# Two superblocks of 2 x 2 quadrants for o and pg over all tokens, with W_o's and W_pg's quadrant sums kept split in DRAM

## The chip, the cores and the metric

The kernel runs on 1 core of one Trainium2 chip. The metric is device time in microseconds (us), measured over the whole execution. Five engines take part: TensorE (PE) for matrix products, with its own sequence of weight loads (PEld); VectorE (DVE), ScalarE (ACT) and GpSimd (POOL) for elementwise work; SyncE (SP), which here only issues DMAs. POOL's queue also issues DMAs, among them those that add into their target (accumulate). The clock that is granted to PE is shown by the profile as a share of full speed (PEclk).

## What is computed

One layer over 2048 prompt tokens and 32 sample tokens with 1024 features, in float32:

```python
z = rmsnorm(x) @ W_in          # q | k | v | gate A | B | C | conv in | conv gate | merge A | merge B
q, k = rope(rmsnorm(q)), rope(rmsnorm(k))        # 8 query heads, 2 key heads of 64
attn = softmax with a sink per head, each chunk of 64 tokens sees itself and 2 chunks before it
yA = (attn * silu(gate_A)) @ W_A                 # 512 -> 1024
yB = (B * conv3(C * u) * silu(gate_C)) @ W_B     # 512 -> 1024
r = x + (sigmoid(mA) * yA + sigmoid(mB) * yB) @ W_o
out = r + sigmoid(r @ W_pg) * (p @ W_pp)         # p has 256 features
```

Besides out, the last rows of k, v and of the conv input are returned.

## The kernel before

Features lie on the 128 partitions and tokens along the free axis. Each float32 operand is split into a high part `hi`, rounded to the matmul format (fp32r), and the rest `lo`; a product is three matmuls, hi·hi, hi·lo and lo·hi, summed in PSUM. The split of a weight piece (128 x 512, 256 KB) is a CAST on ACT and a subtraction on DVE, and the result takes one of `WB` = 5 buffers `w` (hi and lo side by side, 512 KB). Raw pieces come through 8 buffers `wr`.

The program has three phases. Phases 1 and 2 (about 30 to 440 and 440 to 860 us of the span) make `x @ W_in` in two halves of the tokens by Strassen's scheme as Winograd arranges it: 7 products of quadrants in place of 8, for 21 groups of output features. During phase 1, `quad_sums` (L355) loads the four quadrants of W_o and W_pg for each of 4 output rows, makes the 4 sums of quadrants that the scheme needs (products 7, 5, 6 and 3), and stores these 32 sums to DRAM as `qs`, unsplit, for use in phase 3.

Phase 3 (`run_units`, L2247, from about 862 us) works through a list of units written as `plan` (L273 to L287): `yB` and `yA` (products with W_B and W_A, by block of tokens and output row n), `pp` (p @ W_pp for blocks 2 and 3; the others are made earlier), and the two big products `o` (with W_o, key `UO` = 50 in names) and `pg` (with W_pg, `UPG` = 58). Tokens are in four blocks (`BLOCKS`, L23): 512, 512, 512 and 512 + 32, the sample tile being part of the last. o and pg are made in three ways:

- block 0: plainly, 8 x 8 pieces, units `o` and `pg` (`done_o`, `done_pg`);
- blocks 1 and 2: as one superblock (`BIG`, units of kind "B") by the scheme of 7 products, each quadrant 512 features by the 512 tokens of one block; `big_x` makes the 7 combinations of rows, `run_big` the products, `big_done` combines the results and `big_end` finishes a row (for o: add xT by an accumulating DMA and store to `z_r`, the result staying in SBUF as pg's operand; for pg: tanh, times pp, add z_r by an accumulating DMA, store to the output);
- block 3: the same scheme within the block, quadrants of 272 tokens (units of kind "S": `row_quads`, `run_quads`, `quad_done`, `o_quad`, `pg_quad`; tiles `rq`, `s50`, `s58`), in an order of products written out by hand in `last_parts` and `last_pg`.

Attention runs beside the units: 17 tiles of 128 tokens (`attention`, L1330), of two chunks each. A chunk goes through S (scores), E (exp), P (normalised), PT (transposes), O (output); at most two P are live. When the last tile of a block is stored to `z_at`, rows are loaded back (`acf`), split into `ac` and used by yA of that block. The times at which tiles begin are set in a list `begin` (L2300 to L2317), by units of planned PE work.

The order of all this is decided when the program is built: each operation goes through a helper (`call`, L121) that adds its estimated cost (`cost`, L100) to a clock of its engine, `go` starts a generator whose steps become due at such times, and between two matmuls `due` (L172) starts whatever is due and fits in the free buffers (`limit`, L90). PE's own sequence is therefore: units in the order of `plan`, with attention's matmuls put in where they fall due. `next_loads` (L2203) issues weight loads up to 11 pieces ahead (`LOOK`), in the order `worder`, and `split_w` splits them. All operations recorded by the helper have one line in the profile: L135 before, L136 in the changed kernel.

## Time and profile before

| | |
|---|---|
| time, median of 3 runs | 1522.86 us (1521.79 to 1523.18) |
| time of the profiled execution | 1523.18 us |
| its span | 1521.4 us |
| PE, PEld busy | 99%, 88% of the span |
| DVE, ACT, POOL busy | 79%, 55%, 24% |
| DMA from SP's queue | 251.84 MB |
| DMA from POOL's queue | 85.99 MB |
| granted PE clock, mean | 0.993 |

The page lists busy times by engine, the span in slices, the DMA queues, the chain of work that ended last and the costliest groups. Matmuls are pipelined, so a busy share of 99% doesn't say that PE is at its peak: the pitch of instructions in a window in which PE never pauses tells what one costs. A row such as `wr<-qs SPq DMA_DIRECT2D x64, 256.0 KB, 4.8` gives the number of issues, the size of each and the median time from issue to landing. In the view of waits a row names the waiting operation and the engine and tile that it waited for, then the total, the number of times and the longest, in us.

### The profile page before, as it was taken

How to read it: one execution, taken by the hardware profiler on the slowest of the kernel's cores; microseconds unless marked ns; L12 is line 12 of the kernel's file. 1: busy time of each engine (PE TensorE's matmuls, PEld its weight loads, DVE VectorE, ACT ScalarE, POOL GpSimd, SP SyncE). 2: the span in 40 equal slices, each digit the busy share in tenths (PEclk: the TensorE clock that was granted, in tenths of full speed). 3: DMA queues.
4: the chain of work that ended last, by engine and by line, in shares of the span. 5: the costliest groups of instructions: out<-in, count | busy, mean ns of one | idle time of the engine just before them, and what ended most of it. 6: DMA issues, size and time to landing. Idle time of an engine off the chain costs nothing. (4 is left out here: it accounts for less than half of the span.)

```text
span 1521.4 us, 27059 instructions
## 1 busy us (share of the span) xinstructions
PE 1501.7 (99%) x9025; PEld 1334.0 (88%) x9025; DVE 1205.0 (79%) x2291; ACT 835.1 (55%) x1964; POOL 370.3 (24%) x533
## 2 busy tenths in 40 slices
PE   9999999999999999999999999999999999999898
PEld 7878888888889999999999989978888888889898
DVE  7897887875579776898965788789887699786786
...
GB/s 343 152 273 342 310 300 221 286 337 273 245 278 260 322 153 197 110 129 123 153 193 188 254 328 221 221 214 229 193 205 213 240 131 175 275 171 298 272 309 258
DMA packets 207004, 357.39 MB, mean 235 GB/s; under 512 B 24592, under 2 KB 61520, under 8 KB 206864
## 3 DMA queue, kind: packets, MB, share of 16 engines
q1 hardware_dynamic: 164928, 251.84, 51.0%
q0 software_dynamic: 32288, 85.99, 19.6%
...
HBM read 238.21 MB, written 117.46 MB: 234 GB/s over the span
## 5 line engine op out<-in xcount | busy, mean ns | idle before, releaser
L599 PE MATMUL a<-x_l,w 128*128 128x264 f32 (+1 forms) x744 | 228.2, 319 | 0.0
L597 PE MATMUL a<-x_h,w 128*128 128x264 f32 (+1 forms) x744 | 227.2, 320 | 0.0
L602 PE MATMUL a<-x_h,w 128*128 128x264 f32 (+1 forms) x744 | 201.4, 320 | 0.4 <-DVE w L207 0.4
L206 ACT CAST w<-wr 128x512 fp32r<-128x512 f32 (+1 forms) x180 | 110.1, 619 | 104.7 <-PE c L602 28.8
L135 ACT CAST w<-wr 128x512 fp32r<-128x512 f32 x204 | 124.6, 620 | 75.5 <-PE yA L135 17.7
L207 DVE TENSOR_TENSOR w<-wr,w 128x512 fp32r<-128x512 f32 (+1 forms) x180 | 133.8, 753 | 35.2 <-ACT w L206 33.3
L135 DVE TENSOR_TENSOR w<-wr,w 128x512 fp32r<-128x512 f32 x204 | 139.7, 693 | 21.4 <-ACT w L135 18.5
L599 PEld LDWEIGHTS a<-x_l,w 128*128 128x128 f32 x744 | 140.0, 188 | 10.3
L597 PEld LDWEIGHTS a<-x_h,w 128*128 128x128 f32 x744 | 139.7, 188 | 10.4
L135 PE MATMUL b<-xb_h,w 128*128 128x512 f32 x448 | 142.0, 394 | 0.0
L602 PEld LDWEIGHTS a<-x_h,w 128*128 128x128 f32 x744 | 125.2, 188 | 11.2 <-DVE w L207 0.6
L735 PE MATMUL la<-x_h,w 128*128 128x264 f32 x516 | 111.8, 285 | 1.6 <-ACT w L206 1.0
L597 PE MATMUL c<-x_h,w 128*128 128x512 f32 (+1 forms) x336 | 110.5, 339 | 0.1
L599 PE MATMUL c<-x_l,w 128*128 128x512 f32 (+1 forms) x336 | 110.4, 338 | 0.0
L206 ACT CAST w<-a 128x512 fp32r<-128x512 f32 x82 | 49.7, 620 | 95.5 <-DVE a L346 33.2
L602 PE MATMUL c<-x_h,w 128*128 128x512 f32 (+1 forms) x336 | 99.9, 338 | 0.0
L135 PEld LDWEIGHTS b<-xb_h,w 128*128 128x128 f32 x448 | 83.6, 188 | 17.9
L796 DVE SCALAR_TENSOR_TENSOR u<-u,c 128x264 f32<-128x264 f32 (+1 forms) x125 | 59.4, 506 | 43.8 <-ACT u L791 27.3
L135 PE MATMUL yA<-ac_h,w 128*128 128x512 f32 (+1 forms) x320 | 90.4, 360 | 2.3 <-ACT ac_h L135 1.8
L791 ACT COPY u<-a 128x264 f32<-128x264 f32 (+1 forms) x114 | 47.4, 437 | 80.8 <-PE a L602 72.5
L735 PEld LDWEIGHTS la<-x_h,w 128*128 128x128 f32 x516 | 87.0, 189 | 2.2 <-ACT w L206 1.2
L135 PE MATMUL b<-xb_l,w 128*128 128x512 f32 x224 | 88.5, 395 | 0.0
...
## 6 DMA issues: line engine op xcount, KB each, us to landing
wr<-in_wu SPq DMA_DIRECT2D x213, 256.0 KB, 4.1
a<-in_wu SPq DMA_DIRECT2D x116, 256.0 KB, 5.1
wr<-ws SPq DMA_DIRECT2D x74, 256.0 KB, 3.4
wr<-qs SPq DMA_DIRECT2D x64, 256.0 KB, 4.8
ws<-a POOLq DMA_DIRECT2D x63, 256.0 KB, 4.0
qs<-a POOLq DMA_DIRECT2D x24, 256.0 KB, 5.8
tb<-z_t SPq DMA_DIRECT2D x24, 256.0 KB, 4.4
z_t<-tb SPq DMA_DIRECT2D x24, 256.0 KB, 4.0
```

The source lines that it names most:

```text
L135: return f(**kw)
L206: nc.scalar.copy(out=hi, in_=src)
L207: nc.vector.tensor_tensor(out=lo, in0=src, in1=hi.bitcast(F32), op=sub)
L597: nc.tensor.matmul(out=ps[:, :cn], lhsT=w[:, 0, k], rhs=x[0][:, c0:c0 + cn], start=first and k == 0, stop=False, skip_group_check=True)
L599: nc.tensor.matmul(out=ps[:, :cn], lhsT=w[:, 0, k], rhs=x[1][:, c0:c0 + cn], start=False, stop=False, skip_group_check=True)
L602: nc.tensor.matmul(out=ps[:, :cn], lhsT=w[:, 1, k], rhs=x[0][:, c0:c0 + cn], start=False, stop=k == 3, skip_group_check=True)
L735: nc.tensor.matmul(out=ps[:, :m], lhsT=w[:, a, k], rhs=r[:, cols], start=q in "ABG" and j == 0 and e == 0, stop=j == 1 and e == 2, skip_gr ...
L791: nc.scalar.copy(out=t[:, c0:c0 + cn], in_=ps[:, :cn])
L796: nc.vector.scalar_tensor_tensor(out=t[:, c0:c0 + cn], in0=t[:, c0:c0 + cn], scalar=-1.0, in1=ps[:, :cn], op0=mul, op1=sub)
```

## The change

All tokens now go through superblocks: blocks of 512, 512, 528 and 528 tokens (the sample tile stands between prompt tiles 11 and 12, at the border of the two last blocks, and belongs to both), and two superblocks s = 0 (blocks 0 and 1, 512 wide) and s = 1 (blocks 2 and 3, 528 wide, each product in two parts of 264). The plain units `o`, `pg` and the quadrants within block 3 are removed. yB comes for all four blocks first (each W_B piece once), then pp for blocks 2 and 3, then yA, o and pg of superblock 0, then those of superblock 1. Pieces of W_A and W_pp are loaded raw and split for each block that uses them. The order of products is changed so that the results chain differently: product 6 gives c12, product 7 takes it from there to c21, and so on (`BO`, `BIG_AFTER`). In s = 1 the last rows of pg add r from SBUF ("rs") on DVE in place of an accumulating DMA.

`quad_sums` splits each of its 32 sums (a CAST on ACT into a tile of the new tag "kh", a subtraction on DVE in place) and stores both parts, 64 stores; it runs at the steps of groups 3, 5, ..., 17 in place of 1 to 8. At use, `next_loads` loads a sum's two parts with one DMA of 512 KB straight into a buffer `w`, with no split. There are 64 such loads, as many as there were raw loads of sums.

```diff
-BLOCKS = [(0, 512, 0), (512, 512, 0), (1024, 512, 0), (1536, 512, TS)]
+BLOCKS = [(0, 512), (512, 512), (1024, 528), (1552, 528)]
+TILES = [(P * i, P) for i in range(12)] + [(T3, TS)] + [(T3 + TS + P * i, P) for i in range(4)]
-W = 512 + TS
+W = 532
...
-    BIG = (1, 2)
-    BO = {UO: (2, 7, 1, 6, 5, 3, 4), UPG: (1, 7, 6, 5, 3, 2, 4)}
...
+    BO = {UO: (2, 1, 6, 7, 5, 3, 4), UPG: (1, 6, 7, 5, 3, 2, 4)}
+    NA = [((4, 5, 6, 7, 0, 1, 2, 3), (0, 4, 1, 5, 2, 6, 3, 7))[b % 2] for b in range(NB)]
+
+    def products_of(s_, x):
+        def pairs_of(p, r):
+            return [("B", s_, x, n, v) for e in (0, 2) for v in (p, r) for n in (e, e + 1)]
+        out = {p: [("B", s_, x, n, p) for n in range(4)] for p in (2, 7, 4)}
+        out[5] = pairs_of(5, 3)
+        if x == UPG:
+            out[1] = pairs_of(1, 6)
+        else:
+            out.update({p: [("B", s_, x, n, p) for n in range(4)] for p in (1, 6)})
+        return [v for p in BO[x] if p in out for v in out[p]]
+
+    plan = [("yB", b, n) for n in range(2) for b in range(3)] + [("yB", 3, n) for n in range(2)]
+    plan += [("yB", b, n) for n in range(2, 8) for b in range(4)]
+    first, second = products_of(0, UO), products_of(1, UO)
+
+    def mixed(b, parts):
+        ys = [("yA", b, n) for n in NA[b]]
+        return ys[:6] + [parts[0], ys[6], parts[1], ys[7]] + parts[2:]
+
+    pps = [("pp", 3, n) for n in range(8)]
+    plan += [("pp", 2, n) for n in range(8)] + pps[:4] + [("yA", 0, n) for n in NA[0]]
+    plan += first[:4] + pps[4:] + mixed(1, first[4:8]) + first[8:] + products_of(0, UPG)
+    plan += [("yA", 2, n) for n in NA[2]] + second[:4] + mixed(3, second[4:8]) + second[8:] + products_of(1, UPG)
...
-    quad_sum = {(x, n): dram.tile([P, 4, 4, P], F32, tag=f"qs{x}_{n}", name=f"qs{x}_{n}") for x in (UO, UPG) for n in range(4)}
+    quad_sum = {(x, n): dram.tile([P, 4, 2, 4 * P], F32, tag=f"qs{x}_{n}", name=f"qs{x}_{n}") for x in (UO, UPG) for n in range(4)}
...
         for p, o in ((7, "sc"), (5, "a21"), (6, "a11"), (3, "a12")):
-            nc.gpsimd.dma_start(out=quad_sum[x, n][:, WS[p]], in_=t[o])
+            h, lo = high(f"qh{p}_{x}_{n}"), t[o].bitcast(F32R)
+            split(h, lo, t[o])
+            nc.gpsimd.dma_start(out=quad_sum[x, n][:, WS[p], 0], in_=h.bitcast(F32))
+            nc.gpsimd.dma_start(out=quad_sum[x, n][:, WS[p], 1], in_=t[o])
...
-    sums_at = {(0, 1 + 2 * n + e, 6): (x, n) for n in range(4) for e, x in enumerate((UO, UPG))}
+    sums_at = {(0, 3 + 2 * (n + 4 * e), 6): (x, n) for n in range(4) for e, x in enumerate((UO, UPG))}
...
+    def ac_rows(b, j):
+        while b not in ac_open:
+            yield {}
+        yield {"tmp": 1}
+        yield from split_rows(0.5, lambda: ac_pair(b, j), z_at[:, j], ("ac", b, j), b)
...
+        if "rs" in u:
+            eV.tensor_tensor(out=t, in0=t, in1=u["rs"][:, :m], op=add)
...
+        subs = blk(2 * s)[2]
+        floor[0] = 3 * len(subs)
+        fresh = p != 3 and (p != 6 or x == UO)
...
+        for y, (ps, c0, cn) in enumerate(pss):
+            for k in range(4):
+                while ("XB", s, x, p, k) not in have or w_ready.get(wi, 1e9) > now[0]:
                     idle()
...
+                w = wp.tile([P, 2, 4, P], F32R, tag="w", name=f"w{i}")
+                W2[i] = w[:, 0], w[:, 1]
+                fin[0] = 0.0
+                eY.dma_start(out=w.bitcast(F32).rearrange("p a b c -> p a (b c)"), in_=quad_sum[key[2:4]][:, WS[key[4]]])
+                w_ready[i] = fin[0] + 0.5
...
-    e1, e2 = T[f"yA1_{NA[1][0]}"], T["yA3_0"]
+    e1, e2 = T[f"yA1_{NA[1][0]}"], T[f"yA2_{NA[2][0]}"]
+    left.update({0: 4, 1: 4, 2: 5, 3: 5})
+    for e in range(len(TILES)):
+        t = 11 * e if e < 8 else e1 - 30 + (e2 - e1) * (e - 8) / 9
+        begin.append((t, lambda e=e: go(attention(e), None, {"z": 1, "tmp": 2})))
```

In PE's sequence, at the end of the attention of block 1 (chunks 14 and 15 are its last; names are tile, chunk and a running number), these rows stood before, block 0's plain `o0` among them:

```order
L135 MATMUL O_15_13021<-ptl_15_2_12916,VH_10072 128x256
L135 MATMUL o0_3_0_12962<-m0_7_h_12698,w395_12841 128x512
L135 MATMUL pq2_2_13037<-cst_69,zq2_2_12828 128x128 x4
L135 MATMUL pkv2_2_13042<-cst_69,zkv2_2_12830 128x128 x2
L135 MATMUL o0_4_0_13049<-m0_0_h_12298,w396_12868 128x512
L135 MATMUL PT_16_0_13062<-cst_69,P16_12804 128x128 x4
L135 MATMUL PT_16_2_13069<-cst_69,P16_12804 128x128 x2
L135 MATMUL o0_4_0_13049<-m0_0_l_12299,w396_12868 128x512
L135 MATMUL S_18_0_13083<-KH_10068,qs2_1_12983 128x192
```

At the same place in the changed kernel, PE has the next three chunks without other work between them, and then yA of block 1:

```order
L136 MATMUL O_15_13235<-ptl_15_2_13186,VH_10224 128x256
L136 MATMUL PT_16_0_13249<-cst_69,P16_13080 128x128 x4
...
L136 MATMUL S_18_0_13271<-KH_10220,qs2_1_13221 128x192
...
L136 MATMUL O_16_13291<-pth_16_0_13254,VH_10224 128x256
...
L136 MATMUL PT_17_0_13304<-cst_69,P17_13193 128x128 x4
...
L136 MATMUL O_17_13347<-pth_17_0_13309,VH_10224 128x256
...
L136 MATMUL PT_18_0_13361<-cst_69,P18_13270 128x128 x4
...
L136 MATMUL O_18_13389<-ptl_18_2_13372,VH_10224 128x256
L136 MATMUL yA1_0_0_13144<-ac1_0_h_13379,w385_12870 128x512
```

The 512-wide matmuls of o that stood between the chunks are gone from here, and yA1, which stood behind all of block 0's o and pg, follows directly.

On DVE, the last rows of the program (the last combinations of pg's products with pp and with r) were these:

```order
L135 TENSOR_TENSOR e33_3_18105<-e33_3_18105,s58d_3_18302 128x272
L135 SCALAR_TENSOR_TENSOR tg133_3_18235<-tg133_3_18235,pp133_3_18233 128x272
L135 TENSOR_TENSOR tg133_3_18235<-tg133_3_18235,rs133_3_18237 128x272
...
L135 SCALAR_TENSOR_TENSOR tg033_3_18165<-tg033_3_18165,pp033_3_18163 128x272
L135 TENSOR_TENSOR tg033_3_18165<-tg033_3_18165,rs033_3_18166 128x272
```

In the changed kernel they are:

```order
L136 TENSOR_TENSOR c21_158_2_7_18101<-c21_158_2_7_18101,rs2_2_18621 128x528
L136 TENSOR_TENSOR c21_158_3_7_18146<-c21_158_3_7_18146,b158_3_4_0_18724 128x264
L136 TENSOR_TENSOR c21_158_3_7_18146<-c21_158_3_7_18146,b158_3_4_1_18725 128x264
L136 SCALAR_TENSOR_TENSOR c21_158_3_7_18146<-c21_158_3_7_18146,pp2_3_18656 128x528
L136 TENSOR_TENSOR c21_158_3_7_18146<-c21_158_3_7_18146,rs2_3_18658 128x528
```

The last product is combined in two parts of 264, and the steps behind it take a whole row of 528 columns where they took 272.

More of the change, by code (lines that the diff above doesn't have):

```diff
@@ L1382, in attention @@
             eS.copy(out=h, in_=src)
-        if last and i >= 3:
+        if out:
             vo = tmp(f"vo{i}", cols=P)
@@ L1412, in attention @@
         yield {"ps": 2, "qs": 1}
-        if last and i >= 3:
+        if out:
             ko = kso[P - TS:P] if sample else kpo
@@ new lines, in big_unit @@
+            if s and (n == 3 and p in (2, 4) or p == 4):
+                loads.append(("rs", z_r[n + 4 * i]))
+        units.append(dict(b=2 * s + j, n=n, p=p, x=x, s=s, kind="B", name=f"b{s}{x}_{n}_{p}", w=[("B", s, x, n, p)],
+                          act=[()] * 4, loads=loads, got=0))
+    def run_big(u):
+        s, x, n, p = u["s"], u["x"], u["n"], u["p"]
+        g = big[s, x, n]
+        subs = blk(2 * s)[2]
+        floor[0] = 3 * len(subs)
+        fresh = p != 3 and (p != 6 or x == UO)
+        if not fresh:
+            while ("e", s, x, n, {6: 1, 3: 5}[p]) not in have:
+                idle()
+        if fresh:
+            pss = []
+            for e, (c0, cn) in enumerate(subs):
@@ L2079, in run_quads @@
                 banks[0] += 1
-                g[new] = bank(f"s{x}{new}_{n}")
-        for k in range(4):
-            for (n, p), wk in zip(u["parts"], u["w"]):
-                wi = w_of(wk, u)
-                i, half = XP[p]
-                while ("X", x, i, k) not in have or w_ready.get(wi, 1e9) > now[0]:
+                pss.append((bank(f"b{s}{x}_{n}_{p}_{e}"), c0, cn))
+            if p in (1, 5):
+                g["a"] = pss
+        else:
+            pss = g["a"]
+        wk, = u["w"]
@@ L2091, in run_quads @@
-                if k == 3 and p in (1, 5, 6):
-                    hold[0] = now[0] + 0.2 + SEM + 3 * (0.00044 * m + 0.0064)
-                for e, (w, r) in enumerate(((hi, xs[0]), (hi, xs[1]), (lo, xs[0]))):
-                    eT.matmul(out=ps[:, :m], lhsT=w, rhs=r, start=fresh and k == 0 and e == 0, stop=k == 3 and e == 2,
-                              skip_group_check=True)
-                    due()
-                if k == 3:
-                    w_over(wk)
-        for n, p in u["parts"]:
-            go(quad_done(x, n, p), now[0] + SEM, None, -1)
+                xh, xl = XB[s, x, p, k]
@@ new lines, in run_big @@
+                for e, (w, r) in enumerate(((hi, xh), (hi, xl), (lo, xh))):
+                    while begin and begin[0][0] <= work[0]:
+                        begin.pop(0)[1]()
+                    eT.matmul(out=ps[:, :cn], lhsT=w, rhs=r[:, c0:c0 + cn], start=fresh and k == 0 and e == 0,
+                              stop=k == 3 and e == 2, skip_group_check=True)
+                    work[0] += 0.00044 * cn + 0.0064
+                    due()
+                if n == 3 and y == len(pss) - 1:
+                    free("k", 2)
+                    free("kx", 2)
@@ L2169, in tile_hybrid_stream_step @@
     room = {"w": WB - len(W2), "wf": 8}
-    n_load, to_split, landed = [raws[0]], list(range(len(made), raws[0])), {i: 3.0 for i in range(raws[0])}
-    room["wf"] -= len(to_split)
+    n_load, n_split, landed = [raws[0]], [len(made)], {i: 3.0 for i in range(raws[0])}
+    room["wf"] -= raws[0] - len(made)
     def w_of(key, u):
```

681 lines of the change are left out of this document (176 added, 505 removed).

## The prediction

> **What bounds the kernel now.** I read the busy shares first, then TensorE's (PE's) list of waits, then windows.
>
> ```profile
> span 1521.4 us, 27059 instructions
> PE 1501.7 (99%) x9025; PEld 1334.0 (88%) x9025; DVE 1205.0 (79%) x2291; ACT 835.1 (55%) x1964; POOL 370.3 (24%) x533
> ```
>
> PE is busy for all but 20 us, so the time is the sum of its instructions, plus the few places where it stops. The execution took 1523.18 us, 1.8 more than its span; the median of the runs is 0.3 below it. What an instruction costs is its pitch, read where PE never pauses. The next rows hold start and end, then busy time with instruction counts for PE, its weight loads (PEld), DVE, ACT and POOL, then the granted clock, the DMA share and GB/s.
>
> ```profile
> 160.00:200.00 40.00, 40.00 (x175) 32.43 (x174) 32.30 (x53) 15.92 (x35) 11.85 (x24) 1.00 0.90 311
> 600.00:640.00 40.00, 40.00 (x331) 40.00 (x330) 29.42 (x57) 16.11 (x36) 11.09 (x16) 1.00 0.34 106
> 1441.00:1470.00 29.00, 29.00 (x234) 29.00 (x233) 23.13 (x46) 19.87 (x41) 5.21 (x6) 1.00 1.02 302
> ```
>
> The first holds 512-wide matmuls, 40.00/175 = 228.6 ns each; the second 264-wide ones, 120.8 ns; the third 272-wide ones, 123.9 ns. Two halves of 264 cost 241.6 ns, so half a superblock of 528 columns costs 13 ns more than one of 512. Where PE stops is in the next two views: waits (total, times, longest), and windows at the attention output of block 0 and at the start of the quadrants of block 3.
>
> ```profile
> PE s50a L135 <- DVE w L135: 2.5, 1, 2.5
> PE yA L135 <- ACT ac_h L135: 1.8, 2, 1.3
> PE s50b L135 <- DVE w L135: 1.4, 1, 1.4
> ...
> 995.00:1010.00 15.00, 11.91 (x48) 8.15 (x46) 9.56 (x23) 10.52 (x31) 0.00 (x0) 0.66 0.50 163
> 999.40:1009.70 10.30, 9.19 (x26) 6.02 (x27) 5.14 (x11) 5.88 (x17) 0.00 (x0) 0.50 0.30 115
> 1420.00:1440.00 20.00, 15.38 (x99) 14.40 (x98) 17.62 (x34) 10.87 (x22) 2.62 (x3) 0.83 0.80 228
> 1440.00:1500.00 60.00, 59.33 (x468) 58.54 (x467) 51.54 (x102) 41.09 (x87) 12.07 (x14) 1.00 0.99 305
> ```
>
> The list shows single waits of 1 to 2.5 us; the windows show what they cost with the clock that falls behind them. At 995 to 1010, PE is idle for 15.00 - 11.91 = 3.1 us, and of the 9.19 busy us at clock 0.50 half, 4.6, is lost: **7.7 us**. At 1420 to 1440, 99 matmuls at 123.9 ns are 12.3 us: **7.7 us** lost; in the 60 us after it 468 are 58.0: **2.0 us**.
>
> **The matmuls.** Counted in the order of both kernels, 624 of 512 columns and 1152 of 272 go, 2304 of 264 come: block 0's plain o and pg (384 of 512) fall under the scheme, while blocks 2 and 3 turn 528 wide. At the pitches: -142.6 - 142.7 + 278.3 = **-7.0 us**. The arithmetic saved for block 0 is nearly all spent on the 264-wide halves. Here the Trainium skill speaks: "TensorE: Matmul & The Clock Gate", section "Wait — 56ns, not 53.3ns?", gives columns / 2.4 GHz + about 2.5 ns for the start of one matmul to the next. By it this term would be an estimated -8.9 us. The rows say 120.8 ns for 264 columns against its 112.5, with the weight loads busy for the whole window, so the measurement decides.
>
> **The stops that go.** The quadrants (rq rows, s50, s58) are removed, with their 9.7 us. The wait at block 0's yA hangs on this chain:
>
> ```profile
> 986.22 0.28 PE L135 MATMUL O<-ptl,VH 128*128 128x256 f32 x1
> ...
> 986.99 0.56 SPq L135 DMA_DIRECT2D z_at<-at  x1
> ...
> 993.62 0.38 SPq L135 DMA_DIRECT2D acf<-z_at  x1
> ...
> 998.70 0.63 ACT L135 ACTIVATE ac_h<-acf 128x512 fp32r<-128x512 f32 x1
> ...
> 999.39 0.79 PE L135 MATMUL yA<-ac_h,w 128*128 128x512 f32 x1 [1.35 <-ACT ac_h L135]
> ```
>
> From the last O matmul of chunk 7 (986.5) to the first yA it takes 12.9 us, through a store and a load. Before, PE has between these two 6 matmuls of 512, 28 of 272 and 49 narrower ones, about 10.3 us. After, it has 72 of 264 and the same 49: 72 x 0.1208 + 5.5 = 14.2 us. So this wait should go: **-7.7 us**.
>
> **The stop that comes.** Block 1's attention is now wanted by yA1 long before it was. In the changed order PE has, from chunk 14's transposes (PT_14) to the first yA1 matmul, 135 instructions, none wider than 264, with PT_15 to PT_18 and O_14 to O_18 among them: at most 135 x 0.1208 = 16.3 us. Before, 162 matmuls of 512 of block 0's o stood from PT_14 to PT_18, 37 us. How fast can chunks run? These groups (count, busy us, mean ns, idle before) are what ACT does for 32 of them, by instruction:
>
> ```profile
> L135 ACT ACTIVATE E<-S,nm 128x193 f32<-128x193 f32 x120 | 49.3, 422 | 3.4 <-DVE nm L135 3.0
> L135 ACT ACTIVATE P<-E,se 128x192 f32<-128x192 f32 x120 | 46.9, 450 | 7.4 <-DVE se L135 7.3
> L135 ACT ACTIVATION_READ_ACCUMULATOR E<-S,nm 128x1 f32 x128 | 26.1, 204 | 0.0
> L135 ACT CAST pth<-PT 128x512 fp32r<-128x512 f32 x31 | 18.3, 589 | 22.7 <-PE PT L135 22.1
> L135 ACT CAST pth<-PT 128x256 fp32r<-128x256 f32 x31 | 11.9, 384 | 0.6 <-PE PT L135 0.6
> L135 ACT COPY S<-cst 128x2 f32<-128x2 f32 x64 | 9.3, 165 | 18.3 <-PE S L135 15.1 <-DVE w L135 2.6 <-DVE ptl L135 0.3
> ...
> 1146.59 0.38 PE L135 MATMUL PT<-cst,P 128*128 128x128 f32 x2
> ...
> 1152.69 0.27 PE L135 MATMUL PT<-cst,P 128*128 128x128 f32 x1
> ```
>
> They sum to 161.8 us, 5.1 per chunk, which bounds the pace from below. The densest two chunks, 1146.59 and 1152.69, stand 6.1 apart without a pause of PE. Four intervals and about 4 us from the last PT to its O's end (an estimate: two casts, a subtraction and nine matmuls from such rows) give 4 x 5.1 + 4 = 24.4 to 4 x 6.1 + 4 = 28.4 us for work worth 16.3: a stop of 8 to 12 us. ACT also casts weights and K, q rows there, so I take the upper part, **+11**. The 12.9 us from O_15 to yA1's operand run beside chunks 16 to 18. Bounds: 0, if the chunks run ahead, to 24, if all goes at half clock.
>
> With pauses of some us per chunk the clock may fall as it did at 999.40: half of 6 us, **+3**, from 0 to 5. The Trainium skill, "TensorE: Matmul & The Clock Gate", section "What's actually happening", has the gate drop to 4/8 after an idle window of about 3.4 us and open after a busy one. By that rule gaps shorter than this cost no clock, and the sum would be 3 us less; the row agrees on the half, though its 10.3 us are about three such windows.
>
> **Rows between o and pg.** In both superblocks pg's operands wait for the last o product: eviction, accumulate from xT, store to z_r, subtraction, split.
>
> ```profile
> L135 DVE TENSOR_TENSOR w<-wr,w 128x512 fp32r<-128x512 f32 x204 | 139.7, 693 | 21.4 <-ACT w L135 18.5 <-PE b L135 1.5
> L135 ACT CAST w<-wr 128x512 fp32r<-128x512 f32 x204 | 124.6, 620 | 75.5 <-PE yA L135 17.7 <-PE b L135 14.5 <-PE yB L135 11.1
> ...
> c<-in_xT POOLq DMA_DIRECT2D x16, 256.0 KB, 6.8
> z_r<-c SPq DMA_DIRECT2D x16, 256.0 KB, 4.9
> ```
>
> That is 6.8 + 4.9 and four operations of some 0.7, 14.5 us, with queueing 17. The new order has six or seven products (2.7 to 2.9 us each) in between, where there were eight: 17.4 us or more. Cover is thin: **+3** for both, from 0 to 6.
>
> **Splits and stores.** The 64 casts and 64 subtractions on the sums at use go (39.7 us of ACT, 44.4 of DVE), covered by PE wherever it didn't stop: 0. The 32 splits in phase 1 fall on these rows:
>
> ```profile
> 280.00:320.00 40.00, 40.00 (x175) 32.45 (x174) 35.80 (x58) 14.55 (x25) 12.96 (x25) 1.00 0.81 283
> 320.00:360.00 40.00, 40.00 (x174) 32.44 (x173) 26.68 (x45) 18.41 (x32) 11.42 (x22) 1.00 0.93 323
> ```
>
> A step of quad_sums takes DVE four additions and now four subtractions, about 5.6 us, and moves 12 pieces of 256 KB per two groups (some 80 GB/s over 40 us). On 35.80 busy of 40 that is 41.4: **+1**, from 0 to 5. The stores leave by POOL's queue and nothing waits for them till phase 3.
>
> The 64 loads of split sums carry 512 KB each. The nearest row is 4.8 us for 256 KB:
>
> ```profile
> wr<-qs SPq DMA_DIRECT2D x64, 256.0 KB, 4.8
> ```
>
> Between 4.8 and 9.6 us, they are under the 11 us that four other buffers of w give (four products of 2.8): 0, up to 6 if the queues are as full as at 1440 (share 0.99).
>
> **The end.** The last products close with these instructions, and now at 528 columns:
>
> ```profile
> 1516.08 0.29 PE L135 MATMUL s58a<-rq_h,w 128*128 128x272 f32 x1
> ...
> 1516.41 0.40 ACT L135 ACTIVATE tg<-s58a 128x272 f32<-128x272 f32 x1 [0.60 <-PE s58a L135]
> 1516.91 0.43 DVE L135 SCALAR_TENSOR_TENSOR tg<-tg,pp 128x272 f32<-128x272 f32 x1
> 1517.38 0.44 DVE L135 TENSOR_TENSOR tg<-tg,rs 128x272 f32<-128x272 f32 x1
> ...
> L640 ACT ACTIVATE u<-u 128x528 f32<-128x528 f32 x16 | 10.5, 653 | 5.2 <-DVE u L796 5.2
> L684 DVE SCALAR_TENSOR_TENSOR u<-tg,u 128x528 f32<-128x528 f32 x8 | 5.6, 695 | 0.0
> L751 DVE TENSOR_TENSOR o<-o,la 128x264 f32<-128x264 f32 x42 | 17.7, 422 | 11.3 <-PE la L735 11.3
> ```
>
> One more addition of 264 (0.42), tanh 0.65 for 0.40, two DVE operations of about 0.70 for 0.43 and 0.44, and half a microsecond for a store of twice the size (estimate): **+1.7**, from 1 to 3.
>
> **The sum.** 1521.4 - 7.0 - 9.7 - 7.7 + 11 + 3 + 3 + 1 + 1.7 = 1516.7; with 1.8 around the span 1518.5, by the median 0.3 less: **1518 us**. Certain items give -24, new waits take back 20: the result hangs on how many of those come.
>
> **Rivals.**
> - *Attention keeps up.* PT_14 and its followers may be ready early, since chunks before them stand 8 to 10 us of PE work apart and only two are in flight. Then stop and clock cost 3 instead of 14, and the transitions 0: 1504 to 1510, say 1506. Against it: ACT's 5.1 us per chunk on 16.3 us of work.
> - *Attention paces a starved PE: slower.* With only narrow matmuls to fill, PE idles in every chunk, the clock goes to 0.50, and PT, S and O, which are links of the chunk's own chain, take twice as long. From about 7.7 us per chunk (1.9 over the 5.8 that +11 stands for) the time passes before's by 0.2%; at 9 us and half clock to the end the stop is 24 and the clock 5: 1518 + 15 = 1533 (1526 to 1538). For it: half clock lasted 10.3 us behind a shorter wait. Against: two chunks at 6.1 us.
> - *Memory.* Phase 1 beside its full DVE and DMA, and the 512 KB loads, at their upper bounds: +10, 1526.
> - *The order doesn't do what it says* has little room: the rows of the order show the split sums loaded straight into w.
>
> **Chances.** Forecast 0.50 (1511 to 1525), attention keeps up 0.20, starved PE 0.22, memory 0.08. A measurement of this kernel can tell about 0.2%, 3 us: faster is below 1519.8, slower above 1525.9. Of the forecast's half, 0.28 lies below 1519.8 and 0.20 between: faster 0.48; same 0.20 plus 0.03 of the others; slower 0.29. The range takes half of the first rival and most of the second: 1506 to 1533.
>
> **What would show it.** Right: counts and pitches as given; no wait at yA0 and a gap of 8 to 12 us, some at clock 0.50, between PT_14 and yA1; no stop of several us after 1400; 6.5 to 7.5 us from the last matmul to the end. Wrong: PE pausing in phase 1, at the weight loads of the last stage, or between o and pg for over 3 us each; or no gap at yA1.

## The result, and the profile after

The changed kernel is slower. Its median is 1561.99 us over 4 runs (1552.74 to 1564.68) against 1522.32 us over 4 runs of before (1518.87 to 1523.18): a ratio of 1.0254, with a 95% interval of 1.0208 to 1.0300. The prediction was 1518 us, in a range of 1506 to 1533: wrong in its sign, and 44 us too low. The profiled execution took 1563.18 us.

The head of the changed kernel's page gives the span, then busy time, share and instructions of each engine:

```profile
span 1561.4 us, 27885 instructions
PE 1510.0 (97%) x9553; PEld 1361.0 (87%) x9553; DVE 1207.0 (77%) x2302; ACT 802.6 (51%) x1905; POOL 388.6 (25%) x566
```

PE is busy 8 us longer and idle for 51 us where it was idle for 20. DVE is as busy as before and ACT less so: nothing got heavier on the whole, but PE now stands and waits. Windows over phase 1, phase 2 and phase 3 tell where (busy time and count for PE, PEld, DVE, ACT, POOL, then granted clock, DMA share, GB/s). Of the changed kernel:

```profile
20.00:440.00 420.00, 405.61 (x1723) 324.71 (x1722) 325.43 (x535) 194.31 (x367) 130.36 (x241) 0.98 0.80 282
440.00:860.00 420.00, 414.21 (x3258) 406.46 (x3257) 333.10 (x667) 211.28 (x453) 115.84 (x168) 0.99 0.58 188
860.00:1570.00 710.00, 673.57 (x4512) 616.88 (x4510) 537.06 (x1082) 382.12 (x1061) 137.12 (x144) 0.98 0.82 238
```

Of before, the first of these stretches:

```profile
20.00:440.00 420.00, 419.90 (x1826) 339.87 (x1825) 327.28 (x537) 190.38 (x359) 117.86 (x218) 1.00 0.80 281
```

In the same 420 us of phase 1, PE gets through 103 matmuls fewer; at 228.6 ns each that is 23.5 us. This stretch holds the largest part of the miss, and it was priced at +1.

To add up losses I use one measure, "pauses": the time from the start of one matmul to the start of the next beyond 6 ns plus 0.435 ns per column (228.7 ns at 512 columns, 120.9 at 264), summed over a stretch. Half clock counts in it, and so does what attention's narrow matmuls take beyond that line in every kernel, so only differences between kernels mean something. Before has 7.8, 8.2 and 51.0 us in the three stretches (the last to the end), the changed kernel 30.9, 14.1 and 69.8. Together with the first 20 us (7.2 and 5.9) that is 74.2 and 120.7, or +46.5; the span less the pauses fell from 1447.2 to 1440.7, or -6.5; the sum is the +40.0 of the span.

These are PE's largest waits in the changed kernel (total, times, longest):

```profile
PE a L595 <- ACT u L789: 7.8, 2, 4.3
PE b L595 <- ACT w L207: 6.3, 1, 6.3
PE O L136 <- DVE ptl L136: 5.0, 4, 3.5
PE la L733 <- ACT x_h L207: 3.3, 1, 3.3
PE pq L136 <- DMA zq<-z_q: 3.0, 1, 3.0
PE b L136 <- DVE xb_l L136: 2.7, 3, 2.3
PE b L136 <- ACT xb_h L136: 2.3, 1, 2.3
PE pp L136 <- DVE tt L136: 2.2, 2, 1.7
```

The waits of before on `s50` and `s58` are gone, as forecast, and no wait of yA on `ac` is left among the large ones. In their place stand single waits of 2 to 6 us, most of them at places that the prediction didn't name.

**Phase 1.** The first two rows are two places in the trace. The timeline of the changed kernel there (start, duration, engine, line, operation, in brackets the idle time before it and what ended it):

```profile
264.14 8.00 SPq L540 DMA_DIRECT2D b<-in_xT  x4
272.23 0.45 SPq L325 DMA_DIRECT2D wr<-in_wu  x1
...
279.38 0.62 ACT L207 CAST w<-wr 128x512 fp32r<-128x512 f32 x1 [9.13 <-DMA wr<-in_wu]
...
280.05 0.80 PE L595 MATMUL b<-x_h,w 128*128 128x512 f32 x1 [6.28 <-ACT w L207]
...
312.77 1.14 ACT L207 CAST w<-a 128x512 fp32r<-128x512 f32 x2 [7.60 <-DVE a L337]
313.82 0.58 ACT L789 COPY u<-a 128x512 f32<-128x512 f32 x1
314.45 0.79 PE L595 MATMUL a<-x_h,w 128*128 128x512 f32 x1 [4.34 <-ACT u L789]
```

At 264 SP's queue spends 8 us on four loads of x rows, which wait for buffers that a DMA has yet to release (5.2 us of it for the store of a conv row, 1.1 for that of a sum). The weight load behind them in the same queue leaves only at 272.23, so its cast at 279.38 comes after 9.13 us without work on ACT, and PE waits 6.28 us. At 312.77 it is ACT's own order that blocks: casts of weights wait 7.60 us for a sum on DVE (L337), and the eviction of PE's accumulator (`u<-a`) is queued behind them. In both places an instruction that waits holds up another that has nothing to do with it. A third stop, of 3.4 us up to 340.0, is like the second. By pauses the three are 6.5, 4.5 and 3.6 us, and the half clock that comes with them adds some 8.5: together the 23.1 us by which phase 1 is longer than before's. The cost isn't spread over the phase; it is three collisions of queues.

**Phase 3.** The stop at yA1 came as described. From the first transpose of chunk 14 to the first yA matmul (timeline, then the window between the two and a part of it):

```profile
1091.45 0.60 PE L136 MATMUL PT<-cst,P 128*128 128x128 f32 x4
...
1118.48 0.45 PE L136 MATMUL yA<-ac_h,w 128*128 128x512 f32 x1
```

```profile
1091.40:1118.50 27.10, 21.64 (x138) 19.04 (x136) 19.34 (x45) 22.26 (x80) 4.10 (x5) 0.87 0.59 180
1107.70:1114.50 6.80, 6.60 (x28) 6.16 (x29) 3.93 (x10) 5.41 (x21) 0.00 (x0) 0.50 0.65 188
```

27.1 us for 138 instructions that are worth at most 138 x 0.1208 = 16.7 (forecast 24.4 to 28.4 us for 135 worth 16.3). ACT is busy for 22.26 of it, and the clock is at half for 6.80 us of it. Another stop, unforeseen, is at 1320 to 1360:

```profile
1320.00:1360.00 40.00, 36.48 (x247) 34.07 (x246) 28.69 (x57) 20.56 (x55) 10.93 (x13) 0.96 1.08 319
```

```profile
1354.58 0.43 DVE L136 SCALAR_TENSOR_TENSOR tk<-tk,yA 128x264 f32<-128x264 f32 x1 [6.30 <-DMA tk<-z_t]
1354.93 0.68 DVE L136 TENSOR_TENSOR ptl<-PT,pth 128x512 fp32r<-128x512 f32 x1
...
1355.67 0.39 PE L136 MATMUL O<-ptl,VH 128*128 128x256 f32 x1 [3.52 <-DVE ptl L136]
```

The DMA queues are full (1.08, 319 GB/s); DVE stands for 6.30 us at the gating of yA's result, whose `tk` has not landed; attention's subtraction `ptl` stands behind it in DVE's order, and PE waits 3.52 us for that. No wait of PE for the gating itself is among those listed.

The end of the program, by the timeline:

```profile
1554.98 0.28 PE L136 MATMUL b<-xb_h,w 128*128 128x264 f32 x1
...
1556.16 0.64 ACT L136 ACTIVATE c<-c 128x528 f32<-128x528 f32 x1 [2.20 <-DVE c L136]
1556.84 0.71 DVE L136 SCALAR_TENSOR_TENSOR c<-c,pp 128x528 f32<-128x528 f32 x1 [0.71 <-ACT c L136]
1557.58 0.71 DVE L136 TENSOR_TENSOR c<-c,rs 128x528 f32<-128x528 f32 x1
```

From the start of the last matmul to the end of the span it is 6.4 us, where it was 5.3.

### The profile page after: what moved, and what is told of

It is laid out like the page before. It is cut to its first block, busy times and chain, and to the rows that moved or that the text cites. A ratio compares the mean times of both kernels' runs of the same rounds, so it can differ in the third digit from the quotient of the medians.

```text
span 1561.4 us, 27885 instructions
## 1 busy us (share of the span) xinstructions
PE 1510.0 (97%) x9553; PEld 1361.0 (87%) x9553; DVE 1207.0 (77%) x2302; ACT 802.6 (51%) x1905; POOL 388.6 (25%) x566
## 4 chain that ended last, share of the span: by engine, by line
PE 37%; DVE 5%; DMA 5%; ACT 3%; issue 2%; SPq 0%; DVEq 0%; ACTq 0%; POOLq 0%
PE b L136 16%; PE yA L136 5%; PE yB L136 5%; PE S L136 1%; PE O L136 1%; DMA tk<-z_t 1%; DVE c L136 1%; PE la L733 1%; PE a L595 1%; PE a L597 1%; PE a L600 1%; PE PT L136 1%; PE pp L136 1%; PE lc L733 1%; DMA c<-z_r 1%
## 5 line engine op out<-in xcount | busy, mean ns | idle before, releaser
L136 PE MATMUL b<-xb_h,w 128*128 128x264 f32 (+1 forms) x1344 | 310.4, 323 | 2.3 <-ACT xb_h L136 2.3
L136 PEld LDWEIGHTS b<-xb_h,w 128*128 128x128 f32 x1344 | 223.1, 189 | 20.7 <-ACT xb_h L136 2.8
L595 PE MATMUL a<-x_h,w 128*128 128x264 f32 (+1 forms) x744 | 231.4, 324 | 7.8 <-ACT u L789 7.8
L136 PE MATMUL b<-xb_l,w 128*128 128x264 f32 (+1 forms) x672 | 217.3, 323 | 2.7 <-DVE xb_l L136 2.7
L600 PE MATMUL a<-x_h,w 128*128 128x264 f32 (+1 forms) x744 | 204.7, 324 | 0.3 <-DVE w L208 0.3
L595 PEld LDWEIGHTS a<-x_h,w 128*128 128x128 f32 x744 | 141.8, 191 | 19.6 <-ACT u L789 8.8
L136 PEld LDWEIGHTS b<-xb_l,w 128*128 128x128 f32 x672 | 126.7, 189 | 13.1 <-DVE xb_l L136 3.8
L600 PEld LDWEIGHTS a<-x_h,w 128*128 128x128 f32 x744 | 127.0, 191 | 12.6 <-DVE w L208 1.4
L136 ACT CAST w<-wr 128x512 fp32r<-128x512 f32 x108 | 66.0, 620 | 95.6 <-PE b L136 45.9
L136 PE MATMUL yA<-ac_h,w 128*128 128x264 f32 (+1 forms) x384 | 92.3, 328 | 0.6 <-ACT ac_h L136 0.6
L136 PE MATMUL yB<-ycs_h,w 128*128 128x264 f32 (+1 forms) x384 | 91.0, 327 | 0.0
L207 ACT CAST w<-a 128x512 fp32r<-128x512 f32 x82 | 49.0, 620 | 74.3 <-DVE a L337 29.1
L794 DVE SCALAR_TENSOR_TENSOR u<-u,c 128x264 f32<-128x264 f32 (+1 forms) x125 | 59.4, 508 | 35.4 <-ACT u L789 22.8
```

The source lines that it names most:

```text
L136: return f(**kw)
L207: nc.scalar.copy(out=hi, in_=src)
L595: nc.tensor.matmul(out=ps[:, :cn], lhsT=w[:, 0, k], rhs=x[0][:, c0:c0 + cn], start=first and k == 0, stop=False, skip_group_check=True)
L600: nc.tensor.matmul(out=ps[:, :cn], lhsT=w[:, 1, k], rhs=x[0][:, c0:c0 + cn], start=False, stop=k == 3, skip_group_check=True)
L794: nc.vector.scalar_tensor_tensor(out=t[:, c0:c0 + cn], in0=t[:, c0:c0 + cn], scalar=-1.0, in1=ps[:, :cn], op0=mul, op1=sub)
```

## The experiments

All were timed against before on the same chip. Ratios are with their 95% intervals. Pauses are those of the profiled execution in the three stretches. Each variant's order is laid out anew, so single differences of 2 or 3 us of pauses say little. Two of the kernels, e1 and e5, came out as one and the same program (see below): their medians are 2.6 us apart, and their pauses differ by 0.2, 2.7 and 5.0 us. Runs of the changed kernel scatter over 12 us, so comparisons with it are no better than that.

| kernel | us | ratio to before | pauses 20-440, 440-860, 860-end |
|---|---|---|---|
| before | 1522.32 | | 7.8, 8.2, 51.0 |
| changed | 1561.99 | 1.0254 [1.0208, 1.0300] | 30.9, 14.1, 69.8 |
| e1_early_split | 1548.77 | 1.0170 [1.0153, 1.0187] | 23.0, 6.2, 72.5 |
| e2_late_unsplit | 1567.42 | 1.0290 [1.0273, 1.0307] | 14.8, 10.2, 89.9 |
| e3_early_unsplit | 1557.70 | 1.0230 [1.0214, 1.0245] | 10.0, 8.8, 89.2 |
| e4_before_late | 1526.98 | 1.0035 [1.0024, 1.0046] | 13.8, 7.6, 50.5 |
| e5_split_two_steps_later | 1546.20 | 1.0161 [1.0146, 1.0176] | 22.8, 8.9, 67.5 |
| e6_split_in_phase_2 | 1551.50 | 1.0199 [1.0182, 1.0216] | 9.7, 20.9, 71.8 |
| e7_phase_2_and_plan | 1553.76 | 1.0208 [1.0188, 1.0229] | 9.7, 20.9, 76.7 |
| e8_early_double_stores | 1545.01 | 1.0149 [1.0134, 1.0164] | 20.4, 7.3, 67.3 |
| f1_stores_on_act | 1552.21 | 1.0189 [1.0172, 1.0207] | 29.4, 9.7, 62.8 |
| f2_one_store_of_512k | 1548.87 | 1.0168 [1.0151, 1.0185] | 25.4, 6.4, 67.8 |
| f3_pp_on_dve | 1555.67 | 1.0210 [1.0190, 1.0230] | 23.1, 7.7, 75.8 |
| f4_before_split_sums | 1564.91 | 1.0277 [1.0245, 1.0309] | 24.1, 8.9, 74.3 |
| g1_split_late_phase_2 | 1555.69 | 1.0223 [1.0206, 1.0241] | 9.5, 19.6, 78.4 |
| g2_tiny_second_store | 1541.98 | 1.0131 [1.0097, 1.0165] | 14.9, 10.9, 66.1 |
| h1_phase_2_split_delayed | 1552.20 | 1.0217 [1.0182, 1.0251] | 9.7, 26.7, 65.8 |

### What of phase 1 is the split, what its place

Three variants of the changed kernel, and one of before. e1 makes the sums at the steps where before makes them:

```diff
-    sums_at = {(0, 3 + 2 * (n + 4 * e), 6): (x, n) for n in range(4) for e, x in enumerate((UO, UPG))}
+    sums_at = {(0, 1 + 2 * n + e, 6): (x, n) for n in range(4) for e, x in enumerate((UO, UPG))}
```

> The changed kernel, with the sums of quadrants made at groups 1 to 8 as before the change, still split and stored in two parts. The changed kernel loses 25 us to pauses of PE between 240 and 440 us of its span, where the kernel before lost 3. Theory A (the late steps collide with the preparation of rows for phase 2, from group 7 on, over the temporary buffers and SyncE's queue): the pauses between 240 and 440 fall under 6 us and the time to about 1535 to 1543. Theory B (the splits and doubled stores disturb wherever they stand): pauses of 10 us or more move to 40 to 230 us, and the time stays over 1550.

e2 stores the sums unsplit and splits them at each use, as before did; e3 is e2 with e1's steps:

```diff
-            split(h, lo, t[o])
-            nc.gpsimd.dma_start(out=quad_sum[x, n][:, WS[p], 0], in_=h.bitcast(F32))
-            nc.gpsimd.dma_start(out=quad_sum[x, n][:, WS[p], 1], in_=t[o])
+            nc.gpsimd.dma_start(out=quad_sum[x, n][:, WS[p], 0], in_=t[o])
...
+                eY.dma_start(out=t.rearrange("p a b -> p (a b)"), in_=quad_sum[key[2:4]][:, WS[key[4]], 0])
```

> The changed kernel with the sums stored unsplit, in 32 stores, still at groups 3 to 17, and split at each use in phase 3 as before the change. Theory A: the pauses between 240 and 440 stay at 12 us or more. Theory B: they fall under 6 us. Both: in phase 3 ACT and DVE get 64 casts and 64 subtractions more, where PE has slack of a few us only in the attention stretch: 0 to +8 us there.

> Both at once: phase 1 is that of the kernel before, only phase 3 is changed. Both theories: pauses between 240 and 440 near 3 us and between 440 and 500 near 4 us, so 27 us less than the changed kernel but for what phase 3 pays for the splits; 1534 to 1545.

e4 is before with its sums, unsplit, at the changed kernel's steps:

```diff
-    sums_at = {(0, 1 + 2 * n + e, 6): (x, n) for n in range(4) for e, x in enumerate((UO, UPG))}
+    sums_at = {(0, 3 + 2 * (n + 4 * e), 6): (x, n) for n in range(4) for e, x in enumerate((UO, UPG))}
```

> The kernel before, with only the steps of its unsplit sums moved from groups 1 to 8 to groups 3, 5 to 17. Theory A: pauses of 10 us or more appear between 240 and 440, and the time is 1532 or more. Theory B: within 5 us of the kernel before.

Read as a table of two by two, phase 1's pauses are 10.0 (early, unsplit), 14.8 (late, unsplit), 23.0 (early, split) and 30.9 (late, split). **The split costs 13.0 and 16.1 us, the later steps 4.8 and 7.9.** In before the later steps alone cost 6.0 of pauses, and the time rose by 0.35%, some 5 us. Both causes are real, and the prediction had a price for only one of them, +1. e1 also shows that the small loss of phase 2 hangs on the late steps, with the split: 6.2 instead of 14.1, and 10.2 in e2.

The other side of the same table: in phase 3 the unsplit sums have 89.2 and 89.9 us of pauses, the split ones 72.5 and 69.8. Storing them split takes 17 to 20 us off phase 3. On balance it gains: 8.9 us of time between e3 and e1; the 5.4 between e2 and the changed kernel point the same way, within the latter's scatter. So the edit that did the damage in phase 1 isn't what makes the kernel slower than before. e3, with sums as before has them and where before makes them, is 35 us behind before; by pauses, phase 3 loses 38.2, and the matmuls give some back. So the new order of phase 3, with its sums unsplit, costs more than phase 1 does in any variant. PE's largest waits there in e3:

```profile
PE yA L136 <- ACT ac_h L136: 7.2, 2, 6.6
PE b L136 <- DVE xb_l L136: 6.2, 4, 2.0
PE b L136 <- ACT xb_h L136: 3.2, 2, 1.7
PE pq L136 <- DMA zq<-z_q: 3.1, 1, 3.1
PE b L136 <- DVE w L136: 2.8, 1, 2.8
```

Attention's rows at yA, the operands between products, and a weight: my reading is that the casts and subtractions which the prediction called covered delay those that PE is waiting for.

### Other places and other ways for the split sums

e5 makes each set of sums at e1's steps and asks for its splits and stores two steps later:

```diff
+        if pending and i >= pending[0][0] + 2:
+            quad_splits(*pending.pop()[1:])
...
-            quad_sums(*sums_at[todo[0]])
+            pending.append((i, *sums_at[todo[0]], quad_sums(*sums_at[todo[0]])))
```

> Sums at groups 1 to 8 and split, but the casts, subtractions and stores are issued two products after the loads and additions. With the splits at groups 1 to 8, issued at once, PE paused 23.0 us in 20 to 440 (e1), without them 10.0 (e3). Theory C (ACT's casts of sums stand in its queue before the sums are there, and the casts of weights behind them come late): the pauses fall to 13 us or less and the time by some 10 us below e1's 1548.8. Rival D (the work itself, DVE's subtractions and the doubled stores on full phase 1 engines and queues): they stay at 18 us or more.

e6 moves the whole of it to the changed kernel's own groups 5 to 19 of phase 2, where memory is less used (188 GB/s in the changed kernel's window, 282 in phase 1). e7 does the same and also gives PE more work ahead of yA1:

```diff
-    sums_at = {(0, 3 + 2 * (n + 4 * e), 6): (x, n) for n in range(4) for e, x in enumerate((UO, UPG))}
+    sums_at = {(1, 5 + 2 * (n + 4 * e), 6): (x, n) for n in range(4) for e, x in enumerate((UO, UPG))}
...
-    plan += first[:4] + pps[4:] + mixed(1, first[4:8]) + first[8:] + products_of(0, UPG)
+    plan += first[:8] + mixed(1, pps[4:]) + first[8:] + products_of(0, UPG)
```

> The changed kernel with its eight sum steps moved to phase 2 (at groups 5, 7 to 19), where the windows of the kernel before show 106 GB/s and ACT busy 16 of 40 us. Both C and D: phase 1 as in the kernel with early unsplit sums (10 us of pauses in 20 to 440). C: phase 2 may pause as phase 1 did, by 10 us, since the queue order is the same there; D: under 4 us. Phase 3 as in the changed kernel (70 us of pauses from 860 on, 20 fewer than with unsplit sums). About 1534 to 1538 by D, 1545 by C.

> As the kernel with sums in phase 2, and in the plan of phase 3 the four products 1 of o, which need block 0 alone, come before yA of block 1, with the last four pp units among its ends: 11 us of work move ahead of yA1, 6 us behind it. If the pause at yA1 (14 us over the usual between 1080 and 1120) is chunks 14 to 18 wanted too early, it shrinks by 4 to 6 us net and the time with it; if it is ACT's rate over the whole attention stretch, the pause moves and the time stays within 2 us.

g1 takes the groups after the conv instead (13, 15, 17 and 19, two sets in each), h1 groups 13 to 18 (three sets to a pair of groups) with splits asked for two steps later, as in e5:

```diff
+    sums_at = {(1, 13 + 2 * n, q): (x, n) for n in range(4) for q, x in ((6, UO), (5, UPG))}
```

> The changed kernel with its split sums made in phase 2 at groups 13, 15, 17 and 19, two per group. With groups 5 to 19 (e6) PE paused 3.5 us at each of groups 5, 7, 9, 11, where DVE also makes the convolution, and not at 13 to 19. If phase 1 suffers from its own full memory queues (0.90 to 0.96 share from 100 to 220 us in the kernel with early unsplit sums) and phase 2 at groups 5 to 11 from DVE, then phases 1 and 2 pause about as in the kernel with early unsplit sums (19 us from 20 to 860 all told, 31 in e6) and the time is 1534 to 1540. If a split costs PE its pauses wherever it stands, 30 us remain and the time is 1550.

> The changed kernel with its split sums in phase 2 at groups 13 to 18, three per pair of groups, and the splits issued two products after the loads and additions. In g1, where they follow at once, ACT waited 12.2 us at casts of sums for DVE's additions, with the evictions of PE's banks behind them, and PE paused 29.1 us from 20 to 860 (18.8 in the kernel with early unsplit sums). If the place in ACT's queue is what costs (theory C), the pauses fall to 22 us or less and the time to 1538 to 1546. If it is the work itself (D), they stay at 27 us or more and the time over 1550.

e5 doesn't test its question. In phases 1 and 2 the order on each engine is laid out by a scheduler (`schedule_with_timeline_sim=True` near the kernel's end), and it undid the move. In the traces of e1 and e5 each of DVE, POOL, SP and PE has the same operations on the same tiles in the same order from beginning to end, and so have ACT's 1905 instructions. The casts of the sums wait for them in both; of e1, then of e5 (waits of ACT at 20 to 440):

```profile
ACT qh L207 <- DVE sc L356: 9.2, 5, 2.3
```

```profile
ACT qh L207 <- DVE sc L356: 10.2, 5, 3.0
```

So the 22.8 us after 23.0 say how well a measurement repeats, not whether the bunching of additions and splits matters.

In phase 2, phase 1 is free of the work (9.5 to 9.7), but phase 2 pays: the two stretches together have 30.6, 29.1 and 36.4 us against 18.8 in e3, hence 10 to 18 us in each place tried. In g1 ACT's casts of the sums (`qh`) wait for DVE (waits of ACT at 720 to 880):

```profile
ACT qh L207 <- DVE sc L356: 12.2, 6, 4.4
```

I had taken this for the cause: a cast that stands in ACT's order ahead of its input. h1 was to put the casts well behind their sums, and its phase 2 is worse. But there too they still stand close behind, and wait (560 to 900):

```profile
ACT qh L207 <- DVE sc L356: 9.3, 6, 3.5
```

Whether the place in ACT's queue is the cause in phase 2 is thus not shown either way. What else weighs there is in a window of h1 at 760 to 800:

```profile
760.00:800.00 40.00, 38.71 (x295) 37.78 (x295) 37.97 (x69) 23.23 (x49) 19.70 (x31) 0.95 1.01 376
```

The same window of e3, which has none of this work there:

```profile
760.00:800.00 40.00, 40.00 (x331) 40.00 (x331) 24.21 (x49) 21.41 (x45) 10.76 (x12) 1.00 0.61 196
```

DVE goes from 24 to 38 of 40 us and memory from 196 to 376 GB/s: both are all but full. e7's extra work ahead of yA1 gave nothing: from 980 to 1120 the pauses are 28.5 us, after 28.3 in e6.

### Which part of the split costs: bytes, issues, queue or the arithmetic

e8 stores each sum twice without a split, at e1's steps; g2 stores 16 of 512 columns the second time and reads the first copy twice at use. Both leave the split of the sums out, so o and pg aren't the layer's:

```diff
-            split(h, lo, t[o])
-            nc.gpsimd.dma_start(out=quad_sum[x, n][:, WS[p], 0], in_=h.bitcast(F32))
+            nc.gpsimd.dma_start(out=quad_sum[x, n][:, WS[p], 0], in_=t[o])
...
-            nc.gpsimd.dma_start(out=quad_sum[x, n][:, WS[p], 1], in_=t[o])
+            nc.gpsimd.dma_start(out=quad_sum[x, n][:, WS[p], 1, 0:16], in_=t[o][:, 0:16])
```

> Sums at groups 1 to 8, stored twice unsplit, so 64 stores but no casts and subtractions on ACT and DVE (this leaves the split of the sums out). If the stores on GpSimd's queue and the memory traffic make the pauses, they stay near e1's 23 us in 20 to 440; if ACT and DVE make them, they fall to the 10 us of the kernel without splits, and the time to about 1536.

> As the kernel with unsplit sums stored twice (e8), but the second store of each sum carries 16 of its 512 columns: the 32 further instructions stay on GpSimd's queue, 8.1 of the 8.4 MB go. At use the first slot is read twice, so 512 KB come as before (this leaves the split of the sums out). If the bytes make the pauses (20.4 us from 20 to 440 in e8, 10.0 with single stores), they fall to 12 us or less; if the issues on GpSimd's queue or the order of the queues do, they stay at 17 us or more.

f1 is e1 with the 64 stores on ACT's queue, f2 is e1 with hi and lo side by side in one tile and one store of 512 KB:

```diff
-            nc.gpsimd.dma_start(out=quad_sum[x, n][:, WS[p], 0], in_=h.bitcast(F32))
-            nc.gpsimd.dma_start(out=quad_sum[x, n][:, WS[p], 1], in_=t[o])
+            nc.gpsimd.dma_start(out=quad_sum[x, n][:, WS[p]], in_=hl.bitcast(F32))
```

> Split sums at groups 1 to 8, with their 64 stores issued from ACT's queue in place of GpSimd's. Doubling the stores alone (e8) brought 20.4 us of pauses in 20 to 440 where single stores (e3) had 10.0 and splits with double stores 23.0 (e1). Theory Q (GpSimd's queue: the weight sums' stores and the z stores stand behind the sums' stores, and the buffers that they free come late): the pauses fall to 13 us or less and the time to about 1538. Theory T (the traffic of 8.4 MB more): they stay at 18 us or more. If ACT's queue, which must now wait for DVE's low parts, holds up the casts of weights, they grow.

> Split sums at groups 1 to 8, both parts in one tile and stored by one DMA of 512 KB: 32 issues in place of 64 with the same bytes, still on GpSimd's queue. Q: between e3 and e1, near 13 us of pauses in 20 to 440. T: as e1, 20 us or more.

In phase 1 the pauses go from 10.0 (e3) to 20.4 by a second store alone (e8), and by 2.6 more with casts and subtractions (e1). So **the stores cost more than the arithmetic**, on which the prediction had worked out its +1. Of the 10.4, 5.5 go with the bytes (g2). Windows at 100 to 140 and 140 to 180 show how. Of e3 (one store, unsplit):

```profile
100.00:140.00 40.00, 40.00 (x174) 32.29 (x173) 28.62 (x46) 13.63 (x25) 15.19 (x28) 1.00 0.96 339
140.00:180.00 40.00, 40.00 (x174) 32.38 (x173) 32.00 (x53) 14.31 (x26) 13.45 (x26) 1.00 0.90 315
```

Of e8 (two stores, no split):

```profile
100.00:140.00 40.00, 40.00 (x174) 32.28 (x173) 26.98 (x43) 14.27 (x26) 20.00 (x38) 1.00 1.02 387
140.00:180.00 40.00, 36.15 (x147) 28.77 (x146) 23.55 (x38) 10.52 (x19) 13.94 (x26) 0.91 0.91 336
```

Of g2 (second store of 16 columns):

```profile
100.00:140.00 40.00, 40.00 (x174) 32.30 (x173) 29.80 (x47) 14.88 (x27) 21.12 (x41) 1.00 0.99 341
140.00:180.00 40.00, 40.00 (x174) 32.37 (x173) 30.56 (x48) 13.24 (x23) 19.93 (x39) 1.00 0.95 339
```

Memory is all but full in e3 already, at 339 GB/s and a share of 0.96. The double stores lift it to 387, and in the next 40 us PE falls 27 matmuls behind (147 for 174), 6.2 us. With g2's small stores that stop is gone; DVE and ACT do no less there than in e8. It is most of what e8 loses: PE waits 3.9 us for a cast there, up to 165.1, with the clock at half for 6.8 us around it, and e1 has the like, 5.7 us up to 165.3. The loads of weight pieces fit that: those issued from 60 to 240 us land after 5.5 us in the median in e3 and 5.1 in g2, but after 6.4 in e8 and 6.7 in e1.

The other half of the 10.4 stays open. Fewer issues don't help by themselves: f2, with half as many and e1's bytes, has 25.4, though its loads land after 5.2 us. It has two buffers for the casts where e1 has four, and its casts wait 4.3 us for stores to release them. f1 takes the stores off POOL's queue and has 29.4, but in its ACT queue they must wait for DVE's low parts, so POOL's queue isn't cleared by it.

### Does ACT alone hold up yA1?

f3 is e1 with the 0.5 scaling of pp, some 12 us of work, on DVE:

```diff
-        eS.mul(out=u["pp"][:, c0:c0 + cn], in_=ps[:, :cn], mul=0.5)
+        eV.tensor_scalar(out=u["pp"][:, c0:c0 + cn], in0=ps[:, :cn], scalar1=0.5, scalar2=None, op0=mul)
```

> As e1 (split sums at groups 1 to 8), with the 32 scalings of pp by one half in the attention stretch (399 ns each, 12.1 us of ACT between 1000 and 1120 in the changed kernel) moved from ACT to DVE. If ACT's rate sets the pace of the chunks up to yA1, the pauses from 980 to 1120 (24 us in e1) shrink by 6 to 12 us and the time to 1538 to 1543; if it is the chain of one chunk or DVE, nothing is won or 5 us are lost.

It was 6 us slower than e1 by the ratios, and the loss is in this stretch: from 980 to 1120 the pauses are 34.9 us, after 28.2 in e1, and PE's waits there for attention's subtraction `ptl` on DVE grow from 1.5 to 5.3. So ACT's rate alone isn't the bound; what ACT is spared DVE lacks. With e7's miss it is open what would shorten this stop.

### Would split sums have served before?

f4 is before with split sums, stored in phase 1 and loaded straight into `w`; its own order of units stays:

```diff
+            eY.dma_start(out=w.bitcast(F32).rearrange("p a b c -> p a (b c)"), in_=quad_sum[key[1:3]][:, WS[key[3]]])
```

> The kernel before with its three ways for o and pg, but its 32 sums split in phase 1 and loaded straight into a weight buffer at use, as in the change. Gain: the waits of the quadrants on weights split by DVE, of the 9.7 us at the start of block 3's quadrants some 4 to 9. Cost: what splits and doubled stores cost phase 1, 13 us in e1 against e3. So 1524 to 1532; under 1520 only if phase 1 of the kernel before takes the splits better than that of the changed one.

It loses 2.8%, some 42 us. 16 are in phase 1, as above; 25 are in the quadrants of block 3, whose pauses from 1360 on go from 10.6 to 35.6. PE's largest waits for these loads in f4:

```profile
PE s50a L135 <- DMA w<-qs: 7.4, 5, 3.4
PE s58a L135 <- DMA w<-qs: 7.3, 6, 1.7
PE s50c L135 <- DMA w<-qs: 2.5, 1, 2.5
```

A quadrant product there has 12 matmuls of 272 columns, 12 x 123.9 = 1.49 us, and now wants 512 KB for it, 352 GB/s, beside everything else; the fullest window seen here has 387. In the changed kernel a product lasts 24 x 120.8 = 2.9 us and asks for half of that, and the loads land in 4.6 us in the median. My reading is that the size of the blocks makes split sums bearable.

None of the variants is faster than before. The best that computes the whole is that of e1 and e5, at 1546 to 1549 us.

## Why the prediction was wrong, point by point

The terms of the sum against the profiled execution:

| term | predicted | measured | from |
|---|---|---|---|
| matmuls | -7.0 | -7.6 | span less pauses -6.5, less the end's +1.1 |
| quadrants' stops | -9.7 | -8.9 | pauses from 1360 on: 10.6 to 1.7 |
| wait at yA0 | -7.7 | -8.6 | pauses there |
| stop at yA1 and its clock | +11, +3 | +13.4 | pauses at 1080 to 1120 beyond the usual |
| rows between o and pg | +3 | +2.9 | single pauses at 1239; none at 1473 |
| phase 1 | +1 | +23.1 | pauses |
| phase 2 | 0 | +5.9 | pauses |
| other stops in phase 3 | 0 | +20.0 | the rest of phase 3's +18.8 |
| the end | +1.7 | +1.1 | last matmul to the end |
| first 20 us | 0 | -1.3 | pauses |

The predicted terms sum to -4.7, the measured ones to +40.0. The 44.7 between them are the miss; 28 of it lie in phases 1 and 2 and 20 in stops of phase 3 that were not listed; the other terms take some 3 back.

**Right.** Counts and pitches of the matmuls (the traces have just 624 and 1152 fewer and 2304 more); the quadrants' stops; the wait at yA0; the rows between o and pg; and the stop at yA1, in its place, its 27.1 us and its clock. The rival in which attention keeps up fell with that, and so did the one in which PE starves at half clock to the end.

**The step that failed most: the 32 splits in phase 1 at +1, from 0 to 5.** The prediction added 5.6 us of DVE work to a window in which DVE is busy 35.80 of 40 and took the 1.4 us above 40 for the cost. That asks whether one engine's sum of work fits. The runs showed other prices: 13 us for the split at the early steps (of it 10.4 for the second store alone, half of that for its bytes) and 4.8 to 7.9 for the later steps, which the prediction didn't price at all. Its sentence that nothing waits for the stores till phase 3 holds for their data, not for their buffers (f2's casts wait 4.3 us for them) nor for the memory that they fill: at the early steps the loads beside them, on which PE does wait, land later (6.7 us in e1 for 5.5 in e3). In the changed kernel itself the price was paid at three points in the order of SP's and ACT's queues, which a sum of busy times can't show. The rival "memory" had the right place, and at +10 less than half the size.

**The second step: splits at use "covered by PE wherever it didn't stop: 0".** With the stops of the new order in phase 3 they weren't covered: 17 to 20 us between split and unsplit sums. This error went the other way, since the splits were removed. It means that the structure without them is worse still (e3: 35 us behind before).

**The third: the stop at yA1 and the rows between o and pg as the only new ones in phase 3.** The changed order has several more. At 905.9 PE waits 3.0 us for `zq`, whose load was issued late behind weight loads on SP's queue; at 1025 for a multiplication `tt` of attention's rows on DVE, with ACT busy 36.50 of 40 in the window; at 1158.8, 2.3 us for `xb_h`; at 1351.9 for `ptl`, shown above. Behind all but the second the clock is at half, and they are some 3 to 6 us each by pauses. That they come from narrower work between attention's steps and from fuller queues is my reading of the trace; no run took one of them away alone.

The stop at 1158.8 looks like one between o and pg, but pg begins only at 1229.8. PE has 12 matmuls to a product there, and this wait comes after 105 of them, in o's ninth product: the first product 6, which wants the rows that yA1 has just finished. The prediction looked for thin cover only behind o. There, between o and pg, it was near the mark: one wait of 2.3 us in superblock 0 and none in superblock 1. (Its 17.4 us of cover are six products of 2.9; six of superblock 0's, at 2.7, are 16.2.)

**Another, mis-sized: the end,** +1.1 for +1.7. The half microsecond in it for a store of twice the size stood on no row; from issue to landing the last store took 2.03 us, where before's took 1.80.

The 512 KB loads, at 0 with up to 6, were rightly put: PE nowhere waits for one.

The sentence on the clock went by the trace, and rightly: PE was at half clock from 1107.7 to 1114.5, with no single listed wait over 1.4 us at 1090 to 1125. The Trainium skill, "TensorE: Matmul & The Clock Gate", section "What's actually happening", has the clock at 4/8 after at least one idle window of about 3.4 us. Here a stretch in which PE was only partly busy was enough: in the 3.4 us ahead of the fall it was busy for 1.65.

What stays open: the half of the stores' cost in phase 1 that isn't bytes; what in phase 2 makes the same work cost 10 to 18 us; which part of the new structure makes the most of the 35 us of e3, since it was only run as a whole; and whether the casts' place in ACT's queue matters, since neither e5 nor h1 changed it as meant.
